# A channel mixer of a two-layer encoder by one level of Strassen, with its hidden activations kept in DRAM between two phases

## The chip, the cores and the metric

The kernel runs on one core of one Trainium2 chip. The metric is device time in microseconds (us); before the change it is 2589.34 us, the median of three runs (2588.22 to 2590.02). The engines are named as the profile names them: PE is the matrix engine (PEld its weight load), DVE the vector engine, ACT the scalar engine, POOL the general one, and SP the engine whose queue (SPq) issues the DMA transfers.

## What is computed

Two layers of an encoder on 1024 tokens of width 1024. Each layer is a token mixer (convolution, attention, attention to a memory, one output projection) and then a channel mixer. The change touches the channel mixer alone, and what stands next to it:

```python
x = layer_norm(ALPHA * x + mixed, ln1_g[l], ln1_b[l])
ff = jnp.square(jax.nn.relu(x @ w_up[l])) @ w_down[l]      # w_up 1024 x 4096, w_down 4096 x 1024
x = layer_norm(ALPHA * x + ff, ln2_g[l], ln2_b[l])
```

Everything is float32. The kernel forms a float32 product from three products of parts: each operand is split in a high part `hi` of 12 significant bits and the rest `lo`, and hi·hi, hi·lo and lo·hi are summed in PSUM. So one 128×128×512 block product is three matmuls.

## The kernel before

**Channel mixer.** The 4096 hidden features are 32 chunks of 128, taken in 16 pairs (function `up`, L755 to L777, `down`, L782 to L795, both called from the loop at L801). `up` computes the hidden values of a pair of chunks for both halves of the tokens: for each chunk and half 8 blocks of 128 input features, 3 matmuls each (`mm3`, L106 to L110), so 96 matmuls a pair. The operand that moves is the transposed activation, split in advance (`xm_h`, `xm_l`), 512 tokens wide; the one that stays is the weight. ACT takes the result through the relu and the square (L772, L773), and DVE squares again in full (L774) and subtracts to get the low part (L775). The hidden values `h` stay on chip. `down` multiplies them with the pair's rows of `w_down`: 8 row blocks of 128 tokens, 2 halves of 512 output columns, 6 matmuls each, again 96 a pair; DVE adds each of the 16 results to the row block `y` in SBUF (L795). That is 3072 matmuls of 512 columns for `up` and `down` together in a layer, 6144 in all.

**Weights.** Each 128×1024 piece of a weight is loaded by SP (512 KB, `raw`), ACT makes `hi` (L92), and POOL makes `lo` (L95 on POOL).

**What sets the order.** The program is written as loops, and a scheduler orders the instructions of each engine ahead of time; each engine then runs its list strictly in order. The matmuls of `up` for the next pair and of `down` for the last one are interleaved on PE.

**Ahead of the mixer.** The output projection runs by row blocks of 128 tokens (`wo_ps`, 96 matmuls in each). After each block, DVE adds it to the residual (L744), adds the bias (L745), and normalizes (`ln_row`: L139 to L163); `to_xt` (L186) then turns the row block by 8 transposes on PE (L193) and splits it on ACT and DVE. The turns of the last two row blocks come among the first products of `up`.

**Behind it.** The last two pairs are done row block by row block with the second norm (`fin`, with `ln_row` spread over ACT and POOL for three blocks, `SPREAD`), and each block is stored (L820); in layer 0 it is also turned for the next layer.

Of the kernel before, what the change touches and what calls it, by code (L numbers as in the profile page):

```python
# [14 lines left out]
ALU = mybir.AluOpType  # L15
# [12 lines left out]
NFF = FF // P  # L28
DH = 64
# [18 lines left out]
SPREAD = {1: 1, 3: 1, 5: 1}  # L48
# [4 lines left out]
def encoder(ctx: ExitStack, tc: tile.TileContext, x, memt, w_f, w_v, w_mk, w_mv, w_out, w_up,  # L53
# [52 lines left out]
    def mm3(ps, lhs, rhs, start, stop):  # L106
        """ps += lhs^T rhs, both given as (hi, lo)."""
# [18 lines left out]
    def stats_act(y, name):  # L126
        """Mean and variance of a row, summed by the scalar engine."""
# [37 lines left out]
    def norm_rows(norm, turn, spread, kept):  # L165
        """Norms of the row blocks, each turned when its norm is likely done; the last turns are kept for later."""
# [19 lines left out]
    def to_xt(y, xt, tb, name):  # L186
        """Transposed hi and lo parts of a row block."""
# [14 lines left out]
    off8 = dr.tile([NH, 2048], F32, name="off8")  # L202
    # every row holds the offsets one further on, seen with a pitch of 2048
# [18 lines left out]
    xres = [dr.tile([NTB, P, D], F32, name=f"xres{l}") for l in range(L)]  # L222

# [1 line left out]
    def mem_kv(l, pax, kvd):  # L225
# [10 lines left out]
        # keys and values of one head each, the other head of their chunk zero  # L236
# [35 lines left out]
    def proj(l, chs, xt, evac, after, ws=None, late=()):  # L272
        """A group of feature-major chunks, one half of the tokens after the other."""
# [85 lines left out]
    def conv_norm(l, acc, pax, hf):  # L359
        """Token-major norm over the channels of half of the tokens."""  # L360
# [11 lines left out]
    def conv_out(l, z, pp, pax, mixd, hf):  # L372
        """Back to feature-major, scaled, through the silu."""
# [39 lines left out]
    def mixed(l, tb, m, mixd, om=None):  # L413
        """The hi and lo parts of a row block of the mixer; its last head may still be on chip."""
# [12 lines left out]
    def lam_of(l, pp):  # L427
# [9 lines left out]
        # -(e1 - e2 + li)  # L437
# [473 lines left out]
```

## Time and profile before

| | us |
|---|---|
| median of three runs | 2589.34 |
| span of the profiled execution | 2588.9 |
| PE busy in it | 2451.2 (95%) |
| DVE busy | 1681.4 (65%) |
| ACT busy | 821.5 (32%) |
| POOL busy | 844.8 (33%) |
| channel mixer of layer 0, first to last matmul | 605 to 1313 |
| channel mixer of layer 1, first to last matmul | 1871 to 2572 |

The page of the profile gives busy times by engine, the chain of work that ended last, and the costliest groups of instructions. A row of a group ends in the mean time of one instruction and in the idle time of its engine ahead of it, with what ended that (`<-`). A row of a timeline is start, duration, engine, line, operation, and in brackets the idle time of the engine just before. Consecutive matmuls overlap in the pipeline, so the distance of two starts, not the duration shown, is what one of them costs.

### The profile page before, as it was taken

Reading aid. Unit: us, or ns where it says so; the run is one execution under the profiler, and the core shown is the slowest. Engines: PE = TensorE matmul, PEld = TensorE weight load, DVE = VectorE, ACT = ScalarE, POOL = GpSimd, SP = SyncE. Lnnn points to the kernel's source line nnn. Section 1 sums busy time; section 2 is a strip of 40 time slices with the busy share of each in tenths; the row PEclk is TensorE's granted clock in tenths of the full one; section 3 lists DMA queues with packets and bytes.
Section 4 is the critical chain, followed back from the end, with each engine's and each line's share of the span. In section 5 each row is a group of like instructions: output and inputs, shape, how many; then the busy total and the mean of one; then the engine's idle time right before and its main releaser. Section 6 shows DMA issues by size and latency. Waiting matters only on the chain.

```text
span 2588.9 us, 29858 instructions
## 1 busy us (share of the span) xinstructions
PE 2451.2 (95%) x11912; PEld 2034.0 (79%) x11912; DVE 1681.4 (65%) x2270; ACT 821.5 (32%) x1441; POOL 844.8 (33%) x498
## 2 busy tenths in 40 slices
PE   5999998899999999999999999879999999999997
PEld 3788776678888888888877887767788888888886
DVE  8897789877534453544589868996854435443438
ACT  4212587523222222212222228773222121212111
POOL 5433268413222222222233425582232121212212
PEclk9999999999999999999999999999999999999998
DMA  8334543233111111111123435514221111111101
GB/s 287 114 123 120 177 101 105 84 126 98 49 49 49 49 49 49 50 49 49 59 101 125 136 122 153 142 50 148 67 81 57 41 50 48 49 49 49 49 17 65
DMA packets 68899, 222.51 MB, mean 86 GB/s; under 512 B 7156, under 2 KB 24308, under 8 KB 62068
## 3 DMA queue, kind: packets, MB, share of 16 engines
q1 hardware_dynamic: 68760, 220.61, 26.8%
q8 instruction: 93, 1.52, 0.2%
q14 instruction: 46, 0.38, 0.0%
HBM read 174.41 MB, written 50.36 MB: 87 GB/s over the span
## 4 chain that ended last, share of the span: by engine, by line
PE 71%; DVE 22%; issue 4%; ACT 2%; DMA 1%; SPq 0%; DVEq 0%; ACTq 0%
PE up L110 9%; PE up L108 9%; PE up L109 9%; PE dn L110 9%; PE dn L108 9%; PE dn L109 9%; DVE acc L304 6%; DVE s L496 3%; DVE s L518 3%; PE pj L108 2%; PE pj L109 2%; PE pj L110 2%; PE wo_ps L110 2%; PE wo_ps L109 2%; PE wo_ps L108 2%
## 5 line engine op out<-in xcount | busy, mean ns | idle before, releaser
L795 DVE TENSOR_TENSOR y<-y,dn 128x512 f32<-128x512 f32 x448 | 296.8, 685 | 306.5 <-PE dn L110 304.1
L774 DVE TENSOR_TENSOR r<-r 128x512 f32<-128x512 f32 x128 | 163.3, 1276 | 384.3 <-ACT h L773 383.9
L110 PE MATMUL up<-xm_h,wu 128*128 128x512 f32 x1024 | 400.0, 391 | 0.0
L108 PE MATMUL up<-xm_h,wu 128*128 128x512 f32 x1024 | 399.6, 391 | 0.0
L109 PE MATMUL dn<-wd,h 128*128 128x512 f32 x1024 | 399.1, 390 | 0.0
L109 PE MATMUL up<-xm_l,wu 128*128 128x512 f32 x1024 | 398.9, 390 | 0.0
L110 PE MATMUL dn<-wd,h 128*128 128x512 f32 x1024 | 390.0, 390 | 1.9 <-DVE h L775 1.9
L108 PE MATMUL dn<-wd,h 128*128 128x512 f32 x1024 | 391.4, 391 | 0.0
L95 POOL TENSOR_TENSOR wd<-wd_raw,wd 128x1024 fp32r<-128x1024 f32 x64 | 154.8, 2438 | 539.8 <-ACT wd L92 539.8
L95 POOL TENSOR_TENSOR wu<-wu_raw,wu 128x1024 fp32r<-128x1024 f32 x64 | 157.1, 2457 | 468.7 <-ACT wu L92 468.7
L92 ACT ACTIVATE wd<-wd_raw 128x1024 fp32r<-128x1024 f32 x64 | 64.5, 1054 | 564.5 <-PE dn L110 559.5
L110 PEld LDWEIGHTS dn<-wd,h 128*128 128x128 f32 x1024 | 192.2, 188 | 43.3 <-DVE h L775 2.8
L110 PEld LDWEIGHTS up<-xm_h,wu 128*128 128x128 f32 x1024 | 192.3, 188 | 40.6
L109 PEld LDWEIGHTS up<-xm_l,wu 128*128 128x128 f32 x1024 | 192.5, 188 | 40.3
L109 PEld LDWEIGHTS dn<-wd,h 128*128 128x128 f32 x1024 | 192.4, 188 | 40.2
L108 PEld LDWEIGHTS up<-xm_h,wu 128*128 128x128 f32 x1024 | 192.3, 188 | 40.2
L108 PEld LDWEIGHTS dn<-wd,h 128*128 128x128 f32 x1024 | 192.2, 188 | 39.9
L772 ACT ACTIVATE r<-up 128x512 f32<-128x512 f32 x128 | 76.6, 598 | 428.6 <-PE up L110 428.6
L304 DVE SCALAR_TENSOR_TENSOR acc<-u,pp,acc 128x1009 f32<-128x1009 f32 (+14 forms) x120 | 189.8, 1618 | 0.5
L108 PE MATMUL pj<-x_h,wf 128*128 128x512 f32 x448 | 181.2, 405 | 8.8 <-DVE km L95 5.6
L109 PE MATMUL pj<-x_l,wf 128*128 128x512 f32 x448 | 179.4, 401 | 1.6 <-DVE x_l L95 1.5
L110 PE MATMUL pj<-x_h,wf 128*128 128x512 f32 x448 | 178.3, 399 | 1.9 <-POOL wf L95 1.9
(216 smaller groups left out, 4740.6 us busy)
## 6 DMA issues: line engine op xcount, KB each, us to landing
wu_raw<-in_w_up SPq DMA_DIRECT2D x64, 512.0 KB, 3.5
wd_raw<-in_w_down SPq DMA_DIRECT2D x64, 512.0 KB, 3.7
ks<-kd SPq DMA_DIRECT2D x32, 512.0 KB, 11.0
wf_raw<-in_w_f SPq DMA_DIRECT2D x28, 512.0 KB, 3.6
qd<-stg SPq DMA_DIRECT2D x8, 1024.0 KB, 4.2
qs<-qd SPq DMA_DIRECT2D x32, 256.0 KB, 5.8
kd<-stg SPq DMA_DIRECT2D x8, 1024.0 KB, 3.9
wo_raw<-in_w_out SPq DMA_DIRECT2D x16, 512.0 KB, 3.5
```

The lines of the kernel that those rows point to most:

```text
L92: nc.scalar.activation(hi, src, AF.Copy)
L95: (lo_eng or nc.vector).tensor_tensor(lo, src, f(hi), op=ALU.subtract)
L108: nc.tensor.matmul(ps, lhsT=lhs[0], rhs=rhs[0], start=start, stop=False)
L109: nc.tensor.matmul(ps, lhsT=lhs[0], rhs=rhs[1], start=False, stop=False)
L110: nc.tensor.matmul(ps, lhsT=lhs[1], rhs=rhs[0], start=False, stop=stop)
L304: nc.vector.scalar_tensor_tensor(acc[:, c, a:b], u[:, c, a + t - PAD:b + t - PAD], pp[:, k:k + 1], acc[:, c, a:b], ALU.mult, ALU.add)
L496: nc.vector.tensor_tensor_reduce(out=sc[:, m], in0=ps.rearrange("p a b -> p (a b)"), in1=bt[:, b0:b0 + T], scale=-0.125, scalar=3e38, op0= ...
L518: nc.vector.scalar_tensor_tensor(sc[:, 0], sc[:, 1], st[:, 5:6], sc[:, 0], ALU.mult, ALU.add)
L772: nc.scalar.activation(r, ps, AF.Relu)
L774: nc.vector.tensor_tensor(r, r, r, op=ALU.mult)
L795: nc.vector.tensor_tensor(y[:, cs], y[:, cs], ps, op=ALU.add)
```

## The change

One level of Strassen's scheme (in Winograd's form) splits each operand in four blocks and needs seven block products in place of eight, with sums of blocks ahead and behind.

**Up phase.** The four blocks of the activations are halves of the tokens and halves of the input features; the four of a pair's weights are its two chunks and halves of the input features. Seven forms of the activations, each 512 tokens by 512 features, are made once in a layer: `x11`, `x21`, `x22` are blocks, `xt1` to `xt4` are sums. `forms` (L742 to L758) makes the sums in place in the row blocks on DVE (four operations of 128×512 for each of the last four row blocks) and `turn_form` (L732) transposes and splits each, 28 times 4 transposes in a layer (16 times 4 before). For each pair `up_forms` makes the weights' sums (four operations on DVE) and splits five of them; `up_first` splits the other two as one piece. All the low parts are now made on DVE, and POOL has none. A product is 12 matmuls (4 blocks, 3 each), a pair 84. ACT copies three intermediate results of a pair, DVE makes the four hidden blocks from them (L847), ACT takes these through relu and square (L848, L849), and DVE makes the four sums of them (L883 to L889) that the second phase needs. Seven blocks of 128×512 (256 KB each) a pair are stored to DRAM (`hd`, L853).

**Down phase.** It begins when the up phase has ended. The hidden features are taken in two groups of 16 chunks, each in four quarters q. In a group the seven products come in the order 3, 1, 5, 6, 2, 7, 4; one is 4 quarters by 4 row blocks by 6 matmuls. For each product and quarter `down_forms` takes the sum of the weights where there is one (on DVE, in place in the raw piece), splits it (`wf`), loads two stored blocks of the hidden values (`hr`) and splits them (`hf`). DVE adds the results to the row blocks, 36 times a group. The weights' raw pieces `wd` are four of 2 MB, in the places of `x11`, `x21`, `x22` and `xt1`. The normalized row blocks were stored to DRAM (`xmid`) and are loaded again (`yd`), since the up phase used their places.

The matmuls of 512 columns are 5376 in place of 6144 in the two layers.

```diff
+        def forms(tb):
+            h0, h1 = slice(0, 512), slice(512, 1024)
+            if tb < 4:
+                turn_form(ys[tb][:, h0], "x11", tb)
+                turn_form(ys[tb][:, h1], "x21", tb)
+                return
+            t = tb - 4
+            p, q = ys[t], ys[tb]
+            turn_form(q[:, h1], "x22", t)
+            nc.vector.tensor_tensor(q[:, h1], q[:, h1], q[:, h0], op=ALU.subtract)
+            nc.vector.tensor_tensor(q[:, h0], q[:, h0], p[:, h0], op=ALU.subtract)
+            nc.vector.tensor_tensor(p[:, h0], q[:, h1], p[:, h0], op=ALU.add)
+            nc.vector.tensor_tensor(p[:, h1], p[:, h0], p[:, h1], op=ALU.subtract)
+            turn_form(q[:, h0], "xt1", t)
+            for src, name in ((p[:, h0], "xt2"), (q[:, h1], "xt3"), (p[:, h1], "xt4")):
+                late.append((name, t, src))
...
                 ln_row(y, g, b, f"l1_{l}_{tb}")
+                nc.sync.dma_start(xmid[l][tb], y)
                 ys.append(y)
-                if 0 < tb < NTB - 1:
-                    to_xt(ys[tb - 1], xt, tb - 1, f"l1_{l}_{tb - 1}")
+                if tb:
+                    forms(tb - 1)
...
+            def up_first(p, raw):
+                f1 = wts.tile([P, 2, 1024], F32R, tag="w8", name=f"wu{l}_{p}", bufs=3)
+                split(f1[:, 0], f1[:, 1], raw[0])
+                return {1: (f1[:, 0, 0:512], f1[:, 1, 0:512]), 2: (f1[:, 0, 512:1024], f1[:, 1, 512:1024])}
...
+                w[4] = up_form(p, 4, r2[:, h1])
+                tt(r2[:, h1], r2[:, h0], r2[:, h1], op=ALU.add)
+                tt(r2[:, h0], r1[:, h0], r2[:, h0], op=ALU.subtract)
+                tt(r1[:, h0], r2[:, h1], r1[:, h0], op=ALU.subtract)
+                tt(r1[:, h1], r1[:, h1], r1[:, h0], op=ALU.subtract)
...
+                up(z, 6, w, start=False, stop=False)
+                u2 = copy(z, f"u2_{l}_{p}")
+                up(c, 5, w, stop=False)
+                up(z, 7, w, start=False)
+                u3 = copy(z, f"u3_{l}_{p}")
+                h22 = hidden(p, 2, u3, ALU.add, c)
+                keep(p, 2, h22)
+                between()
+                up(d, 4, w)
+                up(c, 3, w, start=False)
+                h12 = hidden(p, 1, u3, ALU.subtract, d)
+                keep(p, 1, h12)
+                h21 = hidden(p, 3, u2, ALU.add, c)
...
+            for p in range(AHEAD):
+                zs[p] = up_a(p, ws[p])
+                if p == 0:
+                    forms(NTB - 1)
+            for name, t, src in sorted(late, key=lambda x: (x[0], x[1])):
+                turn_form(src, name, t, pu)
...
+                w = pd.tile([P, 2, 2, 512], F32R, tag="wf", name=f"wf{l}_{gr}_{i}_{q}", bufs=4)
+                split(w[:, 0], w[:, 1], v[place[i]])
+                hr = wts.tile([P, 2, 512], F32, tag="raw", name=f"hr{l}_{gr}_{i}_{q}", bufs=3)
+                p0 = 2 * (NQ * gr + q)
+                for n in range(2):
+                    loads.append(nc.sync.dma_start(hr[:, n], hd[p0 + n][:, form_of[i]]))
...
+                split(h[:, 0], h[:, 1], hr)
...
+                for q in range(NQ):
+                    for t in range(4):
+                        down(ps[t], cur[q], t, q == 0 and i not in (6, 7), q == NQ - 1 and i not in (1, 6))
+                    if q == NQ - 1:
+                        for t in range(4):
+                            evict(i, t, ps[t])
...
+                    nxt.append(down_forms(*steps[n + 1], q))
```

**Where the order changes.** Three places follow, in layer 0 (the first digit of a name). First PE behind the last matmul of the output projection. Before, `up0_1_0` is the second chunk's product with the first half of the tokens, `l1_0_7_pt0` and `_pt1` are the transposes of the last row block, `dn0_0_0` is the first product of `down`:

```order
L109 MATMUL up0_1_0_5209<-xm0_l0_4450,wu0_1_5160 128x512
L110 MATMUL up0_1_0_5209<-xm0_h0_4449,wu0_1_5160 128x512
L193 MATMUL l1_0_7_pt0_5239<-ident_76,y0_7_5068 128x128 x4
L193 MATMUL l1_0_7_pt1_5246<-ident_76,y0_7_5068 128x128 x4
L108 MATMUL dn0_0_0_5465<-wd0_0_5315,h0_0_5163 128x512
L108 MATMUL dn0_0_1_5481<-wd0_0_5315,h0_0_5163 128x512
L109 MATMUL dn0_0_0_5465<-wd0_0_5315,h0_0_5163 128x512
```

Now `uz0_0` and `uz0_1` are the first products of pairs 0 and 1, and `y0_7` is the last row block:

```order
L830 MATMUL uz0_0_5215<-x11_0_4604,wu0_0_5205 128x512 x12
L737 MATMUL xt1_0_1_5078<-ident_76,y0_5_4893 128x128 x4
L830 MATMUL uz0_1_5265<-x11_0_4604,wu0_1_5212 128x512 x12
L737 MATMUL x22_0_2_5162<-ident_76,y0_6_4990 128x128 x4
L737 MATMUL xt1_0_2_5173<-ident_76,y0_6_4990 128x128 x4
L737 MATMUL x22_0_3_5247<-ident_76,y0_7_5085 128x128 x4
L830 MATMUL uz0_0_5215<-x21_0_4612,wu0_0_5205 128x512 x12
L830 MATMUL uz0_1_5265<-x21_0_4612,wu0_1_5212 128x512 x12
L737 MATMUL xt1_0_3_5258<-ident_76,y0_7_5085 128x128 x4
L737 MATMUL xt2_0_0_5298<-ident_76,y0_0_4460 128x128 x4
```

Ahead of the last row block's transposes there were 48 matmuls behind the projection, and are 24; and behind it come the transposes of the other sums, twelve times four, which end with `xt4_0_3`, and only then the products 6, 5 and 4 of pair 0, which need all of a form.

Second, DVE at the same place. Before, from the last addition of the last row block's norm (L163 on `y0_7`):

```order
L163 SCALAR_TENSOR_TENSOR y0_7_5068<-y0_7_5068,l1_0_7_rs_5140,l1b0_4460 128x1024
L95 TENSOR_TENSOR xm0_l1_4452<-l1_0_6_pt0_5195,xm0_h1_4451 128x4x128
L95 TENSOR_TENSOR xm0_l1_4452<-l1_0_6_pt1_5202,xm0_h1_4451 128x4x128
L774 TENSOR_TENSOR r0_0_0_5190<-r0_0_0_5190 128x512
L775 TENSOR_TENSOR h0_0_5163<-r0_0_0_5190,h0_0_5163 128x512
L95 TENSOR_TENSOR xm0_l1_4452<-l1_0_7_pt0_5239,xm0_h1_4451 128x4x128
```

Now, from that same addition:

```order
L163 SCALAR_TENSOR_TENSOR y0_7_5085<-y0_7_5085,l1_0_7_rs_5157,l1b0_4458 128x1024
L754 TENSOR_TENSOR y0_2_4620<-y0_2_4620 128x512
L95 TENSOR_TENSOR xt1_0_4982<-xt1_0_2_5173,xt1_0_4982 128x4x128
L95 TENSOR_TENSOR x22_0_4970<-x22_0_3_5247,x22_0_4970 128x4x128
L751 TENSOR_TENSOR y0_7_5085<-y0_7_5085 128x512
L752 TENSOR_TENSOR y0_7_5085<-y0_7_5085,y0_3_4711 128x512
L753 TENSOR_TENSOR y0_3_4711<-y0_7_5085,y0_3_4711 128x512
L754 TENSOR_TENSOR y0_3_4711<-y0_3_4711 128x512
L847 TENSOR_TENSOR h0_0_0_5242<-p1_0_0_5228,uz0_0_5215 128x512
L847 TENSOR_TENSOR h0_1_0_5292<-p1_0_1_5278,uz0_1_5265 128x512
L95 TENSOR_TENSOR xt1_0_4982<-xt1_0_3_5258,xt1_0_4982 128x4x128
L95 TENSOR_TENSOR xt2_0_5297<-xt2_0_0_5298,xt2_0_5297 128x4x128
```

Between the norm of the last row block and the split `wu0_0_6` of the weights that the first product 6 needs there now stand 28 operations of 128×512 (that split counted), of which the eleven first are shown. Before there were four low parts of transposes among the mixer's own work.

Third, SP at the end of the up phase. Before, it loads the weights of the next pairs, and nothing else:

```order
L101 DMA wd0_26_raw_8695<-in_w_down 128x1024
L101 DMA wd0_27_raw_8700<-in_w_down 128x1024
L101 DMA wu0_28_raw_8833<-in_w_up 128x1024
L101 DMA wu0_29_raw_8838<-in_w_up 128x1024
L101 DMA wd0_28_raw_8965<-in_w_down 128x1024
L101 DMA wd0_29_raw_8970<-in_w_down 128x1024
```

Now `wd0_0_3` is the last of four weight pieces of the down phase (2 MB each), `yd0_7` the last row block loaded again, `hd0_15` the stores of the last pair, `hs0_15` its sums, `l2g0` and `l2b0` the second norm's parameters, and `wd0_1_0` and `wd0_1_1` are weights of the second group:

```order
L853 DMA hd0_15_5197<-h0_15_2_7656 128x512
L853 DMA hd0_15_5197<-h0_15_1_7685 128x512
L938 DMA wd0_0_3_7733<-in_w_down 128x1024 x4
L973 DMA yd0_7_7717<-xmid0_94 128x1024
L853 DMA hd0_15_5197<-hs0_15_2_7696 128x512
L853 DMA hd0_15_5197<-hs0_15_0_7694 128x512
L853 DMA hd0_15_5197<-hs0_15_1_7695 128x512
L853 DMA hd0_15_5197<-hs0_15_3_7697 128x512
L179 DMA l2g0_7746<-in_ln2_g 128x1024
L179 DMA l2b0_7748<-in_ln2_b 128x1024
L938 DMA wd0_1_0_8076<-in_w_down 128x1024 x4
L938 DMA wd0_1_1_8081<-in_w_down 128x1024 x4
```

The last stores of the up phase now stand in SP's queue behind 8 MB of weights, whose other pieces `wd0_0_0` to `wd0_0_2` are 14 to 25 rows further up, and 4 MB of row blocks. On chip, `wf0_0_3_1`, which product 3 needs for its second quarter, has the place of the sum `hs0_15_1`, and `wf0_0_3_2` that of `hs0_15_3`.

## Rows read from the trace of the kernel before

**Rows 1.** The page: busy time by engine, and the chain that ended last, by engine:

```profile
PE 2451.2 (95%) x11912; PEld 2034.0 (79%) x11912; DVE 1681.4 (65%) x2270; ACT 821.5 (32%) x1441; POOL 844.8 (33%) x498
...
PE 71%; DVE 22%; issue 4%; ACT 2%; DMA 1%; SPq 0%; DVEq 0%; ACTq 0%
```

**Rows 2.** Windows: stretch, length, busy time of each engine, clock, DMA share, GB/s:

```profile
700.00:900.00 200.00, 200.00 (x881) 165.19 (x880) 88.56 (x112) 38.54 (x52) 45.70 (x19) 1.00 0.15 48
605.00:1313.00 708.00, 706.87 (x3138) 584.37 (x3137) 347.85 (x454) 156.30 (x227) 171.81 (x71) 1.00 0.17 54
1871.00:2572.00 701.00, 700.21 (x3088) 578.55 (x3088) 337.64 (x434) 147.00 (x211) 162.35 (x66) 1.00 0.15 50
```

**Rows 3.** Timeline of PE in the mixer's steady part, six matmuls apart:

```profile
899.78 0.39 PE L108 MATMUL up<-xm_h,wu 128*128 128x512 f32 x1
...
901.14 0.39 PE L108 MATMUL up<-xm_h,wu 128*128 128x512 f32 x1
```

**Rows 4.** Timeline of PE at the mixer's start, eight transposes and what follows:

```profile
610.79 1.03 PE L193 MATMUL l_pt<-ident,y 128*128 128x128 f32 x8
611.58 0.48 PE L108 MATMUL up<-xm_h,wu 128*128 128x512 f32 x1
```

**Rows 5.** DVE's group of residual additions in 560 to 606, the output projection:

```profile
L744 DVE SCALAR_TENSOR_TENSOR y<-y,wo_ps 128x1024 f32<-128x1024 f32 x4 | 4.9, 1222 | 6.4 <-PE wo_ps L110 6.4
```

**Rows 6.** Timeline of DVE behind the output projection of layer 0:

```profile
613.22 1.28 DVE L163 SCALAR_TENSOR_TENSOR y<-y,l_rs,l1b 128x1024 f32<-128x1024 f32 x1
...
620.08 0.68 DVE L95 TENSOR_TENSOR xm_l<-l_pt,xm_h 128x512 fp32r<-128x512 f32 x1
620.68 0.68 DVE L774 TENSOR_TENSOR r<-r 128x512 f32<-128x512 f32 x1
```

**Rows 7.** PE's waits in the mixer of layer 0 (total, times, longest):

```profile
PE dn L110 <- DVE h L775: 1.1, 1, 1.1
```

**Rows 8.** Timeline of PE at an idle stretch of the next projection:

```profile
1334.21 0.50 PE L108 MATMUL pj<-x_h,wf 128*128 128x512 f32 x1 [2.81 <-DVE u L319]
```

**Rows 9.** Windows behind that idle stretch:

```profile
1336.00:1340.00 4.00, 4.00 (x13) 3.11 (x12) 0.00 (x0) 0.00 (x0) 0.00 (x0) 0.63 0.00 0
1340.00:1344.00 4.00, 4.00 (x19) 3.33 (x18) 0.00 (x1) 0.01 (x1) 0.00 (x0) 1.00 0.00 0
```

**Rows 10.** Windows in which the DMA engines are full (last two columns):

```profile
1805.00:1810.00 5.00, 5.00 (x23) 4.07 (x22) 5.00 (x11) 1.79 (x5) 0.00 (x0) 1.00 1.02 410
10.00:20.00 10.00, 8.21 (x14) 2.16 (x15) 8.50 (x14) 5.51 (x11) 2.99 (x1) 1.00 1.01 385
40.00:50.00 10.00, 8.50 (x34) 6.85 (x34) 8.65 (x9) 4.09 (x7) 10.00 (x5) 1.00 1.01 303
```

**Rows 11.** The page: a DMA issue, size of one and median time to landing:

```profile
mixd<-om SPq DMA_DIRECT2D x16, 256.0 KB, 2.4
```

**Rows 12.** Timeline of DVE in the mixer's steady part:

```profile
904.68 0.69 DVE L774 TENSOR_TENSOR r<-r 128x512 f32<-128x512 f32 x1 [3.65 <-ACT h L773]
...
910.92 2.48 DVE L774 TENSOR_TENSOR r<-r 128x512 f32<-128x512 f32 x1 [4.82 <-ACT h L773]
```

**Rows 13.** Timeline of POOL at the same time:

```profile
910.45 2.40 POOL L95 TENSOR_TENSOR wu<-wu_raw,wu 128x1024 fp32r<-128x1024 f32 x1 [10.69 <-ACT wu L92]
```

**Rows 14.** The page: groups of the mixer's work on DVE and ACT:

```profile
L795 DVE TENSOR_TENSOR y<-y,dn 128x512 f32<-128x512 f32 x448 | 296.8, 685 | 306.5 <-PE dn L110 304.1
L774 DVE TENSOR_TENSOR r<-r 128x512 f32<-128x512 f32 x128 | 163.3, 1276 | 384.3 <-ACT h L773 383.9
...
L92 ACT ACTIVATE wd<-wd_raw 128x1024 fp32r<-128x1024 f32 x64 | 64.5, 1054 | 564.5 <-PE dn L110 559.5
```

**Rows 15.** Timeline of the program's end:

```profile
2572.01 0.39 PE L110 MATMUL dn<-wd,h 128*128 128x512 f32 x1
...
2572.74 3.10 DVE L162 SCALAR_TENSOR_TENSOR y<-y,l_mv,l2g 128x1024 f32<-128x1024 f32 x1
...
2580.67 0.68 DVE L795 TENSOR_TENSOR y<-y,dn 128x512 f32<-128x512 f32 x1
```

More of the change, by code (lines that the diff above doesn't have):

```diff
@@ L222, in encoder @@
     xres = [dr.tile([NTB, P, D], F32, name=f"xres{l}") for l in range(L)]
+    xmid = [dr.tile([NTB, P, D], F32, name=f"xmid{l}") for l in range(L)]
     def mem_kv(l, pax, kvd):
@@ L746, in encoder @@
                 ln_row(y, g, b, f"l1_{l}_{tb}")
+                nc.sync.dma_start(xmid[l][tb], y)
                 ys.append(y)
[L748 to L750 removed]
+                if tb:
+                    forms(tb - 1)
         right.close()
         last = l == L - 1
+        hd = [dr.tile([P, 7, 512], F32, name=f"hd{l}_{p}") for p in range(NPAIR)]
@@ L754, in encoder, with down_raw @@
         with ExitStack() as es:
             pd = pool(f"d{l}", es=es)
+            NQ = NPAIR // 4
+            PRODS = (3, 1, 5, 6, 2, 7, 4)
+            form_of = {1: 0, 2: 1, 4: 2, 5: 3, 6: 4, 7: 5, 3: 6}
+            place = {1: (0, 0), 2: (1, 0), 3: (1, 1), 5: (0, 0), 7: (0, 1), 6: (1, 1), 4: (1, 0)}
+            wr = {}
+            def down_raw(gr, q):
+                if gr and q < 2:
+                    r = pd.tile([P, 4, 1024], F32, tag="wd", name=f"wd{l}_{gr}_{q}", bufs=2)
+                else:
+                    r = big.tile([P, 4, 1024], F32, tag="b16", name=f"wd{l}_{gr}_{q}", bufs=4)
+                m0 = 4 * (NQ * gr + q)
+                for i in range(4):
+                    loads.append(nc.sync.dma_start(r[:, i], w_down[l, (m0 + i) * P:(m0 + i + 1) * P, :]))
+                wr[gr, q] = r.rearrange("p (b i) (j d) -> p b i j d", b=2, j=2)
@@ L756, in encoder @@
+            for t in range(NTB):
+                ys[t] = ytile(f"yd{l}_{t}")
+            for q in range(NQ):
+                down_raw(0, q)
+            for t in range(NTB):
+                nc.sync.dma_start(ys[t], xmid[l][t])
             g = bcast(ln2_g[l], D, pd, "g", f"l2g{l}")
             b = bcast(ln2_b[l], D, pd, "b", f"l2b{l}")
[L759 to L778 removed]
@@ L797, in pair @@
-            def pair(m):
-                return [m, m + 1], up([m, m + 1]), down_w([m, m + 1])
-            cur = [0, 1], up([0, 1], late), down_w([0, 1])
-            for m in range(2, NFF - 2, 2):
-                new = pair(m)
-                down(*cur)
-                cur = new
-            fin4 = pair(NFF - 2)
-            xn = None if last else new_xt(f"x{l + 1}")
-            if not last:
-                first = proj_w(l + 1, FIRST)
-            tail = tuple(p + q for p, q in zip(cur, fin4))
@@ L813, in fin, with add @@
-            def fin(tb, spread):
-                down(*tail, [tb])
-                parts = 2 if last and tb == NTB - 1 else 1
-                ln_row(ys[tb], g, b, f"l2_{l}_{tb}", spread, parts)
-                dst = out[tb * P:(tb + 1) * P, :] if last else xres[l + 1][tb]
+            touched = set()
+            def add(t, j, ps, op=ALU.add):
+                y = ys[t][:, 512 * j:512 * j + 512]
+                if (t, j) in touched:
+                    nc.vector.tensor_tensor(y, y, ps, op=op)
+                else:
+                    touched.add((t, j))
+                    nc.vector.scalar_tensor_tensor(y, y, ALPHA, ps, ALU.mult, op)
@@ new lines, in evict, with banks @@
+            def evict(i, t, ps):
+                if i in (1, 2):
+                    add(t, 0, ps)
+                if i in (3, 6, 5):
+                    add(t, 1, ps)
+                if i in (5, 7):
+                    add(t + 4, 1, ps)
+                if i == 7:
+                    add(t + 4, 0, ps)
+                if i == 4:
+                    add(t + 4, 0, ps, ALU.subtract)
+            def banks(which, name):
+                if which == 0:
+                    return [v for n in range(2) for v in (lambda z: (z[:, 0], z[:, 1]))(psum2(f"{name}_{n}"))]
+                return [psum1(f"{name}_{n}") for n in range(4)]
@@ new lines, in down, with done @@
+            def down(ps, fm, t, start, stop):
+                w, h = fm
+                ts = slice(t * P, t * P + P)
+                for n in range(2):
+                    for m, (a, c) in enumerate(((0, 0), (0, 1), (1, 0))):
+                        nc.tensor.matmul(ps, lhsT=h[:, a, n, ts], rhs=w[:, c, n], start=start and n == 0 and m == 0,
+                                         stop=stop and n == 1 and m == 2, skip_group_check=True)
+            def done(t, spread, parts=1):
+                ln_row(ys[t], g, b, f"l2_{l}_{t}", spread, parts)
+                dst = out[t * P:(t + 1) * P, :] if last else xres[l + 1][t]
@@ L818, in fin @@
                 for i in range(parts):
                     cs = slice(i * D // parts, (i + 1) * D // parts)
-                    nc.sync.dma_start(dst[:, cs], ys[tb][:, cs])
-            late = norm_rows(fin, lambda tb: None if last else to_xt(ys[tb], xn, tb, f"l2_{l}_{tb}"), SPREAD, 3)
-            xt = xn
+                    nc.sync.dma_start(dst[:, cs], ys[t][:, cs])
+            steps = [(gr, i) for gr in range(2) for i in PRODS]
+            cur = [down_forms(0, PRODS[0], q) for q in range(NQ)]
@@ L827, in _onehot @@
+            if not last:
+                late = [lambda t=t, xn=xn, ys=ys: to_xt(ys[t], xn, t, f"l2_{l}_{t}") for t in range(4, NTB)]
+                xt = xn
 def _onehot():
```

184 lines of the change are left out of this document (145 added, 39 removed).

## Prediction

> **What bounds the kernel now.** I read the page first: PE is busy for 95% of the span and makes 71% of the chain that ended last, DVE 22%, transfers 1% [rows 1]. The windows then show the stage that the change touches: in both mixers PE is busy for all but about 1 us, at full clock, while DVE has half its time free, ACT and POOL three quarters, and the DMA engines five sixths [rows 2]. PE's only wait in the mixer of layer 0 is 1.1 us [rows 7]. So in these 1409 us a matmul less is its cadence less, as long as nothing else becomes late. The cadence is (901.14 − 899.78) / 6 = 0.2267 us [rows 3]; eight transposes take 611.58 − 610.79 = 0.79 us, about 0.1 each [rows 4].
>
> **What is removed.** 6144 matmuls become 5376: 768 × 0.2267 = −174.1 us. The shapes are the same (128×128 against 128×512), so I keep the cadence. Added are 12 × 4 transposes a layer, 96 × 0.1 = +9.5 us.
>
> **Start of the up phase.** This is the first place where PE has to wait for DVE. A 128×512 operation of DVE costs 0.60 us in a row (620.08 to 620.68), a 128×1024 one 1.2 to 1.3 [rows 5, 6]. During the output projection DVE had 6.4 us of idle time over four blocks [rows 5]. The last blocks now carry three times four sums (7.2 us) and three weight splits that POOL had (3.7 us), so DVE is some 4 us behind when the projection's last matmul ends (call that W). Going through its list with these prices: the last block's own residual, norm and what lies between them is 12 us, so `y0_7` is ready at W + 16. Then come the 28 operations of the order, 16.8 us: the first product 6 can start at about W + 33 to 34. Until then PE has 48 matmuls and 17 groups of four transposes, 10.9 + 6.8 = 17.7 us; it waits twice, for `y0_7` and for the end of the list, 16 us together, where it waited 1.1 before. The clock adds to it: after an idle 2.8 us PE ran at 0.63 for 4 us, 13 matmuls where 19 passed in the next 4 [rows 8, 9], some 1.6 us each time. I take +20 us a layer. The lower end is 10 (DVE not behind at W, and forms made while PE turns others), the upper 25 (sums of the last block that also wait for the store of `xmid`, 2.4 us for a small store [rows 11]).
>
> **From the up phase to the down phase.** Product 3's first weights are split behind the last sums of pair 15: one addition, relu and square, four sums and the split, 0.7 + 1.2 + 2.4 + 1.2 and hand-overs, so PE waits at least 6.5 us. What ends later is a store. The raw weights `wd` may be loaded as `x11`, `x21`, `xt1` and `x22` are used for the last time, 108, 74, 60 and 0 matmuls ahead of the phase's end E, so from E − 24.5 us on. From then until the last sums are stored SP issues 8 MB of weights, 4 MB of row blocks, some 5 MB of hidden blocks: 17 × 1024 × 1024 = 17.8 million bytes. Where the DMA engines were full they moved 410, 385 and 303 GB/s [rows 10]. At 400 that is 44.5 us, so the sums land at about E + 20. `wf0_0_3_1` and `wf0_0_3_2` have the places of two of these sums, so the second quarter of product 3 begins at about E + 23, after 1.05 on ACT [rows 14] and 1.2 on DVE; its 72 remaining matmuls (16.3 us) end at E + 39 to 40, in place of 96 × 0.2267 = 21.8. That is 18 us; with two falls of the clock (1.6 each), +21 a layer. At 303 GB/s it would be 59 us of transfers, a loss of 32 with the clock. Below, 8 us: only the 6.5 us chain and a fall of the clock, if the queue is not full.
>
> The DMA engines of this trace were full at 410 GB/s for 5 us [rows 10]. The Trainium skill, "DMA: Bandwidth & Descriptors" (Specifications), gives about 358 GB/s as the limit of memory for one core; by it the burst would be an estimated 50 us and the loss 5 us a layer greater. The rows go above that figure, so I keep 400.
>
> **The steady parts.** For a pair of the up phase DVE has 17 operations of 128×512 and one of 128×1024, 17 × 0.67 + 1.2 = 12.6 us, against 84 × 0.2267 = 19.0 on PE; ACT has some 10.7 (a 128×1024 one takes 1.05 [rows 14]). In the down phase a group costs DVE 56 splits and 16 sums of 1.22 and 36 additions of 0.69 [rows 14], 113 us, against 672 × 0.2267 = 152. Both queues are strictly in order and wait for PE at each hand-over, which the spare 6 us of a pair cover. The transfers are 2.75 MB in 19 us, 150 GB/s, far under what the rows show. For a few late hand-overs I take +5 us in all; from 0 to 30.
>
> **The ends.** The last product of layer 0 and of layer 1 starts only when its last split is made, behind the additions of the product before: +4 each. The tail of layer 1 was 2588.9 − 2572.0 = 16.9 us, with DVE at 3.10 beside POOL and a last block that took 8.2 from its addition on [rows 15]; now no POOL norm stands in the last three blocks, and DVE (4.6 us a block) keeps up with PE (5.4), so −5. Together +3, from −5 to +10.
>
> **Sum**, against the profiled span: 2588.9 − 174.1 + 9.5 + 40 + 42 + 5 + 3 = 2514.3. The span and the median of 2589.34 differ by 0.4, so I forecast 2515 us. With the ends that are likely together its own range is 2485 to 2550.
>
> **Rivals.** *The stalls are covered.* If the scheduler's order lets PE find work in both places (10 and 8 us, the lower ends), the sum is 2588.9 − 174.1 + 9.5 + 36 = 2460; 2445 to 2485. For it: DVE may be less late at W than I count, and the transfers may be spread by the waits in SP's list. Against: the list of the start shows no product of 512 columns between the twelve late groups of transposes, and the places of the last sums are fixed.
>
> *The burst runs at half the rate.* Blocks of hidden values are rows of 2 KB, and loads and stores are mixed; no row here shows such a mix at full load. At 200 GB/s it takes 89 us and costs some 63 us a layer: 2514 + 84 = 2598, about no change; between, 2560 to 2600. Against it: 303 is the lowest full stretch I saw.
>
> *Slower: DVE's queue becomes the bound of the up phase.* In a pair it takes four results of PE by way of ACT. If at each the queue stands for what it stood in the trace (1.6 us at the projection, 6.4 / 4 [rows 5], to 3.65 in the mixer [rows 12]) and other work cannot pass it, a pair is 12.6 + 4 × 1.6 = 19.0, just PE's time; that is the point from which it decides. At 3.65 it is 27 us, at the middle of both 23, 4 us over PE: 32 × 4 = +128, 2643 us. The same would come of operations at 1.28, as L774's mean is [rows 14]. Against: those waits were of an engine with nothing else to do, and DVE's 2.48 us came beside POOL's 2.40 [rows 12, 13], which has no work in this phase.
>
> The Trainium skill, "SBUF — State Buffer" (SBUF: two separate sides), says that DVE and POOL share a port that one of them holds for a whole instruction, and blocks the other. By it DVE's price here is the uncontended one; the trace agrees, with 0.69 and 2.48 for the same operation at 904.68 and 910.92.
>
> **How the numbers follow.** My forecast 0.66; stalls covered 0.18; half rate 0.08; DVE the bound 0.08. The range 2460 to 2565 leaves out half of the covered case, most of the half rate and the slower case, 2 in 10. A measurement of this kernel tells about 0.2% from no change, 5 us. Faster has the first two, and half of the third: 0.88; within 0.2% 0.03; slower 0.09.
>
> **What would show it.** In the windows of the new profile, 16 steady pairs of 19.0 us with PE full, and products of 21.8; a hole in PE of about 16 us behind each output projection, with DVE full, and one of some 18 us at the end of each up phase, with the DMA share near 1 and PE's wait ended by DVE or a store. If DVE is full in steady pairs while PE waits, the slower rival holds; if the holes are missing, the first. The forecast is wrong if the cadence is not 0.2267 for these operands, or if products of the down phase wait for their loads.

## The result, and the profile after

The changed kernel takes **2526.6 us** (2525.9 to 2532.4), the kernel before 2589.7 on the same chip: a ratio of 0.976 (95% interval 0.9746 to 0.9773). The forecast was 2515, in a range of 2460 to 2565. The profiled span is 2524.2 us, 64.7 less than before. The page of the changed kernel, busy time by engine, the chain by engine, and the costliest group of products and of splits:

```profile
PE 2337.9 (93%) x11240; PEld 1912.6 (76%) x11240; DVE 1909.2 (76%) x2598; ACT 1100.8 (44%) x1849; POOL 537.3 (21%) x370
...
PE 63%; DVE 25%; DMA 5%; issue 4%; ACT 2%; POOL 0%; SPq 0%; DVEq 0%; ACTq 0%; POOLq 0%
...
L1008 PE MATMUL db<-wf,hf 128*128 128x512 f32 x1344 | 326.3, 404 | 24.7 <-ACT wf L92 21.3
```

PE has 672 instructions fewer than in [rows 1], as 768 products less and 96 transposes more make it, and its share of the chain fell from 71% to 63%. The third row's last column says that PE stood idle 24.7 us before products of the down phase, 21.3 of it behind a split of weights on ACT. Transfers went from 1% to 5% of the chain. They are mostly the two passages between the phases: in layer 0 the chain runs through one transfer after the other from 910.9 to 958.8, in layer 1 from 2156.4 to 2196.1. Its last transfers in layer 0 (start, duration, what) and what they release:

```profile
943.65 6.26 DMA hd<-h
...
949.98 8.84 DMA hd<-hs
...
959.05 1.07 ACT wf L92
```

The windows of layer 0 (columns as in [rows 2]) divide the mixer into its start, the steady up phase, the passage between the phases, and the down phase:

```profile
605.00:640.00 35.00, 25.56 (x125) 19.76 (x124) 31.65 (x54) 16.17 (x31) 0.00 (x0) 0.90 0.26 91
640.00:920.00 280.00, 280.00 (x1219) 228.26 (x1218) 176.38 (x260) 146.15 (x245) 0.00 (x0) 1.00 0.45 155
920.00:966.00 46.00, 30.70 (x101) 22.72 (x100) 16.21 (x22) 14.67 (x21) 0.00 (x0) 0.78 1.03 397
966.00:1262.00 296.00, 295.79 (x1278) 238.73 (x1276) 217.16 (x238) 110.48 (x117) 14.77 (x5) 1.00 0.38 126
```

In the first and the third PE lacks 9 and 15 us, and the clock is 0.90 and 0.78; in the third the DMA engines are full. In the second and fourth PE is full at clock 1.00. But the counts there are low: 1219 matmuls in 280 us are one in 0.2297 us, where the prediction kept 0.2267 [rows 3]. The timeline of PE shows it for whole products of the down phase, 96 matmuls each:

```profile
1002.60 22.56 PE L1008 MATMUL db<-wf,hf 128*128 128x512 f32 x96
1025.00 22.56 PE L1008 MATMUL dz<-wf,hf 128*128 128x512 f32 x96
1047.40 12.76 PE L1008 MATMUL db<-wf,hf 128*128 128x512 f32 x54
```

From start to start these are 22.40 us, that is 0.2333 a matmul, with no idle time between.

**The start of the up phase.** The projection's last matmul ends about 603.2 (W). The timeline of DVE behind it:

```profile
603.41 1.22 DVE L776 SCALAR_TENSOR_TENSOR y<-y,wo_ps 128x1024 f32<-128x1024 f32 x1
...
613.73 1.28 DVE L163 SCALAR_TENSOR_TENSOR y<-y,l_rs,l1b 128x1024 f32<-128x1024 f32 x1
...
618.04 0.69 DVE L751 TENSOR_TENSOR y<-y 128x512 f32<-128x512 f32 x1 [0.50 <-DMA xmid<-y]
...
622.59 0.69 DVE L847 TENSOR_TENSOR h<-p,uz 128x512 f32<-128x512 f32 x1 [1.08 <-PE uz L830]
...
635.15 3.10 DVE L95 TENSOR_TENSOR wu<-wu_r,wu 128x512 fp32r<-128x512 f32 x5
```

DVE takes up the last block 0.2 us behind W, not 4 us late, and its norm is done at W + 11.8 (the first and second rows). The list behind it then takes longer than its 28 operations at 0.60, by hand-overs of 0.2 to 1.1 us each with ACT and PE, a store among them (third and fourth rows). PE's first product 6 starts at W + 31.5, in layer 1 at W + 32.9 (its first split on ACT is done then, DVE's at W + 32.6).

**The passage.** The timeline of PE (in square brackets the idle time ahead and what ended it), then the waits of 930 to 965 (total, times, longest), then SP's queue:

```profile
929.11 2.96 PE L830 MATMUL uz<-xt,wu 128*128 128x512 f32 x12
934.76 4.60 PE L830 MATMUL uc<-x,wu 128*128 128x512 f32 x12 [2.68 <-DVE h L847]
942.41 2.07 PE L1008 MATMUL db<-wf,hf 128*128 128x512 f32 x4 [3.05 <-ACT wf L92]
945.38 6.58 PE L1008 MATMUL db<-wf,hf 128*128 128x512 f32 x20 [0.90 <-DVE wf L95]
960.16 0.79 PE L1008 MATMUL db<-wf,hf 128*128 128x512 f32 x1 [8.21 <-ACT wf L92]
```

```profile
ACT wf L92 <- DMA hd<-hs: 16.7, 1, 16.7
...
PE db L1008 <- ACT wf L92: 11.3, 2, 8.2
```

```profile
948.74 2.80 SPq L853 DMA_DIRECT2D hd<-hs  x4
...
955.66 7.96 SPq L938 DMA_DIRECT2D wd<-in_w_down  x8
```

The up phase's last product ends at 939.4. ACT then makes one split, and stands 16.7 us for the store of a sum of pair 15 (`hd<-hs`), since the tile `wf` it is to write has that sum's place. The store lands at 959.05, 19.6 us behind the phase's end. Product 3 takes 37.8 us, 36.3 in layer 1, from its first matmul to that of product 1; 96 matmuls are 21.8 to 22.4.

### The profile page after: what moved, and what is told of

Its sections match the earlier page's. It is cut to its first block, busy times and chain, and to the rows that moved or that the text cites. A ratio compares the mean times of both kernels' runs of the same rounds, so it can differ in the third digit from the quotient of the medians.

```text
span 2524.2 us, 30293 instructions
## 1 busy us (share of the span) xinstructions
PE 2337.9 (93%) x11240; PEld 1912.6 (76%) x11240; DVE 1909.2 (76%) x2598; ACT 1100.8 (44%) x1849; POOL 537.3 (21%) x370
## 4 chain that ended last, share of the span: by engine, by line
PE 63%; DVE 25%; DMA 5%; issue 4%; ACT 2%; POOL 0%; SPq 0%; DVEq 0%; ACTq 0%; POOLq 0%
PE uz L830 13%; PE db L1008 12%; PE dz L1008 9%; DVE acc L305 7%; PE uc L830 6%; PE ud L830 3%; DVE s L497 3%; DVE s L519 2%; PE pj L108 2%; PE pj L109 2%; PE pj L110 2%; PE wo_ps L110 2%; PE wo_ps L109 2%; PE wo_ps L108 2%; DMA hd<-hs 1%
## 5 line engine op out<-in xcount | busy, mean ns | idle before, releaser
L1008 PE MATMUL db<-wf,hf 128*128 128x512 f32 x1344 | 326.3, 404 | 24.7 <-ACT wf L92 21.3
L1008 PEld LDWEIGHTS db<-wf,hf 128*128 128x128 f32 x1344 | 258.7, 193 | 90.9 <-ACT wf L92 23.3
L1008 PE MATMUL dz<-wf,hf 128*128 128x512 f32 x1152 | 270.7, 396 | 0.0
L1008 PEld LDWEIGHTS dz<-wf,hf 128*128 128x128 f32 x1152 | 216.8, 188 | 52.0
L830 PE MATMUL uz<-xt,wu 128*128 128x512 f32 x768 | 190.8, 396 | 6.0 <-ACT wu L92 6.0
L830 PE MATMUL uz<-x,wu 128*128 128x512 f32 x768 | 191.9, 396 | 0.0
L95 DVE TENSOR_TENSOR wu<-wu_r,wu 128x512 fp32r<-128x512 f32 (+1 forms) x192 | 145.7, 777 | 39.8 <-ACT wu L92 39.3
L499 ACT ACTIVATE s<-s,ast 128x1024 f32<-128x1024 f32 x128 | 147.2, 1152 | 57.2 <-DVE ast L497 55.0
L830 PEld LDWEIGHTS uz<-x,wu 128*128 128x128 f32 x768 | 146.4, 191 | 32.2
L847 DVE TENSOR_TENSOR h<-u,uc 128x512 f32<-128x512 f32 x64 | 44.0, 688 | 160.7 <-PE uc L830 134.3
L497 DVE CUSTOM_DVE_ANT_0 s<-sc,bt 128x1024 f32<-128x1024 f32 x128 | 153.8, 1214 | 10.5 <-PE sc L495 9.6
L92 ACT ACTIVATE wf<-wd 128x1024 fp32r<-128x1024 f32 x112 | 116.3, 1042 | 42.3 <-DMA hd<-hs 32.6
```

The lines of the kernel that those rows point to most:

```text
L497: nc.vector.tensor_tensor_reduce(out=sc[:, m], in0=ps.rearrange("p a b -> p (a b)"), in1=bt[:, b0:b0 + T], scale=-0.125, scalar=3e38, op0= ...
L499: nc.scalar.activation(sc[:, m], sc[:, m], AF.Exp, scale=-1.0, bias=st[:, m:m + 1], accum_out=st[:, 2 + m:3 + m])
L830: nc.tensor.matmul(ps, lhsT=a[:, kc], rhs=x[:, c, kc], start=start and kc == 0 and n == 0, stop=stop and kc == 3 and n == 2, skip_group_ch ...
L847: nc.vector.tensor_tensor(h, a, ps, op=op)
L1008: nc.tensor.matmul(ps, lhsT=h[:, a, n, ts], rhs=w[:, c, n], start=start and n == 0 and m == 0, stop=stop and n == 1 and m == 2, skip_group ...
```

## The experiments

Each edit is against the changed kernel, or where said against another experiment. The changed kernel's times to compare with are 2526.6 (median) and 2524.2 (span). The experiments ran on other chips, where the kernel before took 2591.3 to 2593.1 us in place of 2589.7, so a difference from 2526.6 is uncertain by some 2 to 3 us; the ratios are each to the kernel before on the same chip.

**Why a matmul takes longer.** The matmuls have the shapes of before, and PE waits for nothing. What differs between groups is where their operands lie. I took the addresses from the compiled program, and from the traces the mean time from start to start, for each kind of product. Distance is the moving operand's address less the stationary one's, in bytes within a partition, modulo 512:

| kernel | products | distance | us a matmul |
|---|---|---|---|
| before | `up`, `dn`, `pj` | 0 | 0.2273 |
| before | `wo_ps`, by piece of `wo` and row block | 32, 64, 96 | 0.2333, 0.2301, 0.2331 |
| after | `uc` with `x` | 0 | 0.2271 |
| after | `uz` with `x` | 0 | 0.2281 |
| after | `uz`, `ud` with `xt` | 448 | 0.2330 |
| after | `db`, `dz` with `hf` | 448 | 0.2333 |
| after | `db` with `hl`, same phase | 0 | 0.2277 |

Two groups do not fit at once. Products of `uz` with `x` often follow products at 448, and then the first five of their twelve matmuls take 0.2263 to 0.2331 us, the other seven 0.2267. And 36 matmuls of `wo_ps` a layer, in the first row block, lie at distance 0 and took 0.230 in the mean, with PE's waits among them; they are not in the table.

The last two rows rule out the address of the moving operand alone as the cause: it is the same four places of `wf` in both, and only the stationary operand (`hf` or `hl`) lies elsewhere. The table is a correlation all the same; four kernels move the tiles and nothing else. An unused tile ahead of the others in each phase's pool shifts `xt2` to `xt4` and `wf`:

```diff
             pu = pool(f"u{l}_up", es=es)
+            pu.tile([P, 144], F32, name=f"pad_u{l}")
...
             pd = pool(f"d{l}", es=es)
+            pd.tile([P, 144], F32, name=f"pad_d{l}")
```

> The only edit is an unused tile of 576 bytes per partition ahead of the tiles of each of the mixer's two phases; it moves xt2 to xt4 and wf (the operands that move) by 576 bytes, so that they stand at the same place modulo 512 as the operands that stay (wu forms, hf). Theory A: the matmul's cadence depends on the distance of its two operands in SBUF modulo 512; in the changed kernel products with distance 0 run at 0.2271 to 0.2284 us, those with distance 448 at 0.2333. Then the windows 700 to 760 and 1000 to 1100 show 0.227 in place of 0.230 and 0.2333, some 3490 matmuls gain 0.0058 each, 20 us: about 2506. Rival B: the cadence comes from the distance of the two operands in general (one at 65 to 137 KB, one above 144 KB) or from what DVE and ACT do in these phases; both stay, and so do the cadences, 2526 (within 3).

Measured: **2507.0 us** (2500.7 to 2508.6), 0.9669 (0.9656 to 0.9682) of the kernel before, 19.6 under the changed kernel. PE's timeline in the same place, whole products:

```profile
1019.57 21.92 PE L1010 MATMUL dz<-wf,hf 128*128 128x512 f32 x96
1041.33 18.98 PE L1010 MATMUL db<-wf,hf 128*128 128x512 f32 x83
```

21.76 us from start to start, 0.2267 a matmul, as before the change. The stationary operands stay where they were, so their address alone is not the cause either; and the products of `uz` with `x`, which were not moved, fall to 0.2269. The size of the pad narrows the rule down. The other three have 16, 80 and 48 floats in place of 144:

> As e1_pad576 with 64 bytes in place of 576: the distance of the operands becomes 512 (0 modulo 512, not modulo 1024). Theory A with 512 as the modulus: cadence of about 0.227 in the down phase, as with 576. If the modulus is 1024 or 2048: 0.2333 stays.

> As e1_pad576 with 320 bytes: the distance is 256 modulo 512. If only a multiple of 512 helps, the cadence in the down phase stays at 0.2333, which also shows that it is not the move as such that helps; if a multiple of 256 (or 64, 128) suffices, 0.227.

> As e1_pad576 with 192 bytes: the distance of the two operands becomes 128 modulo 256. With distances 0, 256 and 512 the cadence was 0.227 in both phases, with 448 it was 0.2333 (96 and 32 in the output projection too). If the distance has to be a multiple of 128, 0.227 here, some 2505; if of 256, 0.2333 and 2526.

The window of 1000 to 1100, in the order: the changed kernel (distance 448), then the pads that give 0 (576 bytes), 256 (320 bytes) and 128 (192 bytes):

```profile
1000.00:1100.00 100.00, 100.00 (x430) 80.65 (x429) 63.09 (x68) 36.16 (x36) 0.00 (x0) 1.00 0.40 137
```

```profile
1000.00:1100.00 100.00, 100.00 (x443) 82.87 (x442) 63.05 (x66) 36.20 (x37) 0.00 (x0) 1.00 0.42 138
```

```profile
1000.00:1100.00 100.00, 100.00 (x442) 82.86 (x442) 62.81 (x66) 36.18 (x36) 0.00 (x0) 1.00 0.42 139
```

```profile
1000.00:1100.00 100.00, 100.00 (x432) 81.04 (x431) 63.47 (x69) 36.18 (x36) 0.00 (x0) 1.00 0.41 137
```

443 and 442 matmuls in 100 us against 430 and 432. The pad of 64 bytes makes the distance 0 modulo 512 as the one of 576 does, and its time agrees (2506.0); 320 bytes took 2503.5, 192 bytes 2524.9 (single runs each). So at a multiple of 256 bytes, of the distances tried, a matmul costs 0.2267 us, and at 448 it costs 0.2333. At 128 it costs 0.2324 in the down phase of layer 0 and 0.2333 in that of layer 1, at the same distance, so the distance is not all that counts. Why it counts, no run here shows.

**Why the passage costs what it costs.** Here `wf` gets another place: two raw pieces `wd` of the second group, wanted much later, are created first in the pool and take the last sums' places, and `wf` comes to stand on `xt2` to `xt4`.

```diff
+            early = [pd.tile([P, 4, 1024], F32, tag="wd", name=f"wd{l}_1_{q}", bufs=2) for q in range(2)]
...
-                    r = pd.tile([P, 4, 1024], F32, tag="wd", name=f"wd{l}_{gr}_{q}", bufs=2)
+                    r = early[q]
```

> The only edit lets the down phase place its late raw weights (wd of group 1) first, so that wf stands on xt2 to xt4 and no longer on the last sums hs_15 of the up phase; the order on PE, ACT, DVE and SP is the same. Theory A: the stall at the end of the up phase is the wait of wf for the store of these sums, 16.7 us of ACT and 8.2 of PE; without it the second quarter of product 3 follows the first, and a layer gains 9 to 12 us (8.2 + 1 of wait, 1 to 2 of clock): about 2505. Rival B: the loads of the last raw weights, behind the same 17 MB, are as late as the stores; then ACT's wait is ended by a load a few us earlier and the gain is under 4 us a layer, 2519 or more. Rival C: the raw weights of group 1 now wait for the stores, and the loads of product 1 behind them in SP's queue come late: the wait moves to product 1, 2520 to 2530.

Measured: **2510.2 us** (2508.0 to 2512.6), 0.9683 (0.967 to 0.9697). Product 3 takes 25.9 and 26.7 us in place of 37.8 and 36.3, 21.5 less in both layers; the gain is 16.4. PE's timeline:

```profile
945.72 23.05 PE L1009 MATMUL db<-wf,hf 128*128 128x512 f32 x92 [0.90 <-DVE wf L95]
968.61 11.36 PE L1009 MATMUL dz<-wf,hf 128*128 128x512 f32 x48
982.09 0.73 PE L1009 MATMUL dz<-wf,hf 128*128 128x512 f32 x2 [2.12 <-ACT hf L92]
```

```profile
ACT hf L92 <- DMA hr<-hd: 15.8, 1, 15.8
```

The hole of 8.2 us in product 3 is gone, and the wait of ACT for a store with it. (ACT now stands 11.9 us for a load of raw weights, ahead of the fourth split, and PE does not come to need that one earlier.) In its place product 1 waits in layer 0, for a split of hidden values behind a load of them from DRAM: from product 1 to the end the down phase takes 300.8 us, 4.5 more than after the change. So the bytes were not fewer; some of the wait for the burst has moved one product on.

**Both edits together, and more of the same.**

> Both edits, the 576 bytes and the place of wf. If they are independent (one is the cadence inside products, the other a wait between the phases), their gains add: 2526.6 less 20 less 16, 2488 to 2493. If the shorter products make the transfers of the first quarters of product 1 later against PE, part comes back as waits there: 2493 to 2500.

Measured: 2488.5 us (2486.9 to 2490.7), 0.9595 (0.9582 to 0.9608): 38.1 less, against 19.6 + 16.4 = 36.0 for the two alone; by the ratios, 42.7 against 23.6 + 19.9. They are two costs, not one. The next kernel keeps the new place of `wf` and reaches the aligned places with smaller pads in other pools, which also bring the output projection's weights `wo` into place:

```diff
+    sm.tile([P, 16], F32, name="pad_sm")
...
+                if k["qb"] == 5:
+                    heads["w"].tile([P, 8], F32, name=f"pad_w{l}")
```

> e12's place of wf, and the distance of the operands made a multiple of 512 by 64 bytes ahead of all tiles on the left and 32 on the right, so that the output projection (1536 matmuls of 0.2302 to 0.2333) is aligned too. If the distance decides there as well: 1536 x 0.0052 = 8 us less than e12, some 2482; if the projection is held by DVE's norms, which have 1.6 us of slack a block, less than 4.

Measured: 2486.7 us (2483.8 to 2488.6), which can't be told from 2488.5. The projection's matmuls did fall from 0.2321 to 0.2275. But they are 48 in a row block and 768 in both layers, and not the 96 and 1536 that the section on the kernel before and the expectation count: 3.5 us at most. The two projections, from their first matmul to their last, took 203.2 us in place of 204.8 in the kernel with both edits, and PE's idle time in them hardly changed (6.9 in place of 6.5). That DVE's norms hold the projection is not shown.

The last of these kernels delays, in the one just described, the loads of the two early pieces until those of product 5's hidden values have been issued:

```diff
-                    loads.append(nc.sync.dma_start(r[:, i], w_down[l, (m0 + i) * P:(m0 + i + 1) * P, :]))
+                    with (tc.issue_after(loads[-1].ins) if gr and q < 2 else ExitStack()):
+                        loads.append(nc.sync.dma_start(r[:, i], w_down[l, (m0 + i) * P:(m0 + i + 1) * P, :]))
```

> As best1, and the loads of the second group's first raw weights (4 MB) come behind the loads of product 5 in SP's list, no longer ahead of product 1's. In best1 PE waited 3.8 and 2.5 us in product 1's third quarter of the two layers, whose loads stood behind those 4 MB. If these were the cause: 5 us less, 2481 or 2482. If product 1's loads wait for the stores of the last sums anyway: no change, 2486.

Measured: **2476.0 us** (2472.3 to 2480.1), 0.9556 (0.9542 to 0.9569), the fastest here, 50.6 us under the changed kernel. The window of the passage and PE's timeline:

```profile
920.00:966.00 46.00, 39.29 (x155) 31.00 (x154) 26.11 (x29) 17.80 (x23) 0.00 (x0) 0.89 0.92 359
```

```profile
939.55 24.05 PE L1013 MATMUL db<-wf,hf 128*128 128x512 f32 x92 [0.89 <-DVE wf L96]
963.43 21.92 PE L1013 MATMUL dz<-wf,hf 128*128 128x512 f32 x96
985.19 5.15 PE L1013 MATMUL db<-wf,hf 128*128 128x512 f32 x22
```

Product 1 (second row) has no wait, and PE is busy for 39.3 of the 46 us where it was 30.7. From product 1 to the end the layers take 289.5 and 284.9 us, 9.0 less in sum than in the kernel ahead (294.6, 288.8), near the 10.7 between the medians (8.3 by the ratios) and more than the 5 expected.

**How near DVE's queue is to being the bound.** In the changed kernel it is not: in 680 to 880 PE waits for nothing, and the longest waits are the other engines' for PE:

```profile
DVE h L847 <- PE uc L830: 45.5, 11, 4.6
ACT wu L92 <- PE uc L830: 39.3, 11, 4.8
```

Two kernels add work to DVE, the sum `s1` taken again eight times a pair for 28 pairs (8 × 0.60 = 4.8 us a pair), or four times (2.4):

```diff
                 tt(s1, h21, h22, op=ALU.add)
+                for _ in range(8 if p < NPAIR - 2 else 0):
+                    tt(s1, h21, h22, op=ALU.add)
```

> Eight more operations of 128x512 on DVE in each pair of the up phase but the last two (a sum made again, nothing else reads it in between). Theory, DVE has slack in the steady pairs: 12.6 + 8 x 0.6 = 17.4 us a pair against 19.2 of PE, no change within 4 us (2523 to 2530). Rival, the waits at the hand-overs take DVE's slack, so that its queue is near the bound: 1.5 us or more for each of 28 pairs, 2568 or more.

> As e3_dve8 with four more operations a pair in place of eight. In e3_dve8 a pair took 21.2 us, 17.4 of work and 4.0 of waits at hand-overs (2.71 for ACT, 1.31 for PE). Theory, these waits are fixed and work comes on top: 12.6 + 2.4 + 4.0 = 19.0 us, just under PE's 19.2, so no change or up to 0.4 us a pair (2526 to 2538). Rival, each added operation of 0.6 us costs PE its share of what it cost in e3_dve8 (53 us for 224 operations), 26 us: 2552.

Eight: 2579.5 us (2578.0 to 2580.2), +53. Four: 2545.8 (2541.4 to 2550.9), +19, between the two expectations. The window of 760 to 820, with eight and with four, and DVE's timeline with eight:

```profile
760.00:820.00 60.00, 55.93 (x238) 43.78 (x237) 47.33 (x74) 28.88 (x48) 0.00 (x0) 1.00 0.43 144
```

```profile
760.00:820.00 60.00, 57.94 (x250) 46.31 (x249) 42.63 (x65) 30.34 (x51) 0.00 (x0) 1.00 0.41 139
```

```profile
770.79 0.69 DVE L95 TENSOR_TENSOR wu<-wu_r,wu 128x512 fp32r<-128x512 f32 x1 [2.71 <-ACT wu L92]
...
772.79 0.69 DVE L847 TENSOR_TENSOR h<-u,uc 128x512 f32<-128x512 f32 x1 [1.31 <-PE uc L830]
```

DVE has 12.7 us of 60 idle with eight operations more, and 17.4 with four, and yet PE waits. DVE stands once a pair for a split on ACT (2.7 us) and once for PE (1.3), and its list is in order, so the work behind stands too. ACT's next work stands for DVE, and PE twice a pair 0.7 us, once for ACT's copy and once for DVE's addition. With eight a pair takes 21.24 us (gaps of PE end at 763.26 and 784.50), where 84 × 0.23 is 19.3: of 4.8 us added, 1.9 reach the end. With four, the pairs from 718 to 880 take 20.3, and over all 28 pairs the median rose by 0.7 us each. The spare time of the prediction, 6 us a pair, was a difference of busy times; the point at which DVE's queue starts to hold PE lies below 2.4 us of added work a pair. How far below stays open, since the scheduler makes the order anew when operations are added.

**POOL at the start.** Three of the first splits, 1.2 us each on DVE, are given back to POOL:

```diff
-                split(f1[:, 0], f1[:, 1], raw[0])
+                split(f1[:, 0], f1[:, 1], raw[0], nc.gpsimd if p < 3 else None)
```

> The low parts of the first three pairs' first weights go back to POOL, three operations of 128x1024 a layer; DVE's list behind the output projection is 3.7 us shorter. Theory, the start of the up phase is the length of DVE's list: it is 2 to 4 us a layer shorter, 2519 to 2523. Rival, DVE stands while POOL works (2.48 in place of 0.69 us beside it in the trace of before), so the list is as long or longer: 2526 to 2534.

Measured: 2532.6 us (2530.6 to 2534.3), 0.977 (0.9757 to 0.9784), no gain over 0.976. The first product 6 starts at W + 33.8 and 34.5, in place of 31.5 and 32.9. POOL's timeline, then DVE's:

```profile
596.01 8.44 POOL L95 TENSOR_TENSOR wu<-wu_r,wu 128x1024 fp32r<-128x1024 f32 x3 [10.94 <-ACT wu L92]
```

```profile
597.78 1.58 DVE L751 TENSOR_TENSOR y<-y 128x512 f32<-128x512 f32 x1
...
599.96 2.23 DVE L752 TENSOR_TENSOR y<-y,y 128x512 f32<-128x512 f32 x1
...
602.17 3.35 DVE L162 SCALAR_TENSOR_TENSOR y<-y,l_mv,l1g 128x1024 f32<-128x1024 f32 x1
```

While POOL works (596.0 to 604.5), three operations of DVE that take 0.67, 0.69 and 1.27 in the changed kernel take 1.58, 2.23 and 3.35. The Trainium skill, "SBUF — State Buffer" (SBUF: two separate sides), says that the two share a port which one holds for a whole instruction; these rows agree.

## Why the prediction came out as it did

The sign and the size were right, and so was the mechanism but for one term; the median lies 11.6 us above the forecast. By terms, in us for both layers, each against its own matmuls at 0.2267 and transposes at 0.1:

| term | predicted | measured |
|---|---|---|
| 768 matmuls less, 96 transposes more | −164.6 | −164.6 (counts as predicted) |
| start of the up phases | +40 | +33 |
| passage to the down phase | +42 | +45 |
| steady parts, over before's | +5 | +18.5 |
| ends and tail | +3 | +4.5 |
| sum | −74.6 | −63.6 |

The span fell by 64.7; the rest, 1.1, lies outside the mixers.

**The steady parts are the mis-sized term.** The step that failed is "The shapes are the same (128×128 against 128×512), so I keep the cadence". In the up phase a matmul took 0.2300 on average, in the down phase 0.2333; with 2688 each, and a last product with `hl` that has the old cadence, that is 25.7 us, of which 7.2 are what the mixers before were over 0.2267 themselves. The prediction put +5 here for late hand-overs of the queues, and in the steady windows there were none: the whole term is the cadence, and kernels that moved the operands gave it back down to 0.2267. It did name this as what would make it wrong. The row that could have told was in the trace of before: PE's products of the output projection took 0.2301 to 0.2333 with the same shapes, and I read the cadence from one place only. Two rows of PE there, six matmuls apart, 1.40 / 6 = 0.2333 us each:

```profile
600.22 0.39 PE L110 MATMUL wo_ps<-wo,ms 128*128 128x512 f32 x1
...
601.62 0.39 PE L110 MATMUL wo_ps<-wo,ms 128*128 128x512 f32 x1
```

**The start** was right in its end (W + 33 to 34; measured 31.5 and 32.9), by two errors that cancel, so that is luck in part. DVE was not 4 us behind at W but 0.2. And the 28 operations took 20.8 us and not 16.8, as hand-overs lay between them. PE fell in the clock as expected: the granted clock was 0.51 from 615 to 618, its lower level of 1.2 GHz, after PE had been busy for 1.4 of 6 us, and 0.90 in the whole window.

**The passage** was right in mechanism and size: the store landed at E + 19.6 (predicted E + 20), the DMA engines moved 397 GB/s (taken as 400). By the figure of the Trainium skill that the prediction weighed, "DMA: Bandwidth & Descriptors" (Specifications), the burst would have been an estimated 5 us longer; the trace differs from it. Not foreseen was that product 3 of pair 15 stands right behind product 7 and waits 2.7 us for DVE's addition on the bank that it goes on with. These 5.4 us in both layers are more than the 3 over; the rest of the passage was a little cheaper than counted.

**The ends** hide two misses that offset each other: PE stood idle for 2.1 and 0.7 us in the last products of the layers, where +4 each was taken, and the tail behind the last matmul went from 16.9 us to 16.1, where −5 was taken.

**The rivals.** The stalls were not covered: 9 and 15 us of idle PE stand in the two windows. The burst did not run at half rate. DVE's queue was not the bound; the mechanism is real, as eight more operations showed (+53), but its price begins much earlier than the prediction's "6 us a pair" says, and it costs a part of what is added and not the whole.

## What to carry to other kernels

When a change moves operands to other buffers, the cadence of its matmuls has to be read again: in these runs 448 or 128 bytes of distance modulo 512, in place of 0 or 256, cost 2.5 to 3%, and an unused tile of 64 bytes gave it back. A tile that is written first in a new phase should not get the place of one that is stored last in the old phase, and loads that are wanted late should be issued late. Spare time of an engine in a loop of in-order queues is not the difference of busy times: it is found by adding work to it.

## What was not expected of the hardware

That the time of a back-to-back matmul depends on the addresses of its two operands: 0.2267 us where their distance is a multiple of 256 bytes (0, 256), 0.2324 to 0.2333 at 448 or 128, with nothing else changed. In the trace of before the projection shows values between (0.2301 at 64), which fits neither of the two levels and stays unexplained.

And that DVE and POOL are slower together by more than the work that POOL takes over: three splits moved off DVE freed 3.7 us of it, and three of its operations became 4.5 us longer.
